# The first up-projection pair of MLP groups 2 to 6 by seven products instead of eight

## The chip, the cores and the metric

The kernel runs on one core of a Trainium2 chip. The metric is the time of one execution in microseconds (us), the median of several runs. Times inside an execution come from a hardware profile of one execution, the one whose page is shown.

The engines go by the profile's names: PE is TensorE (matmuls; PEld are its weight loads), DVE is VectorE, ACT is ScalarE, POOL is GpSimd, SP issues the DMAs from HBM. SBUF is the working memory, PSUM the eight banks that matmuls write. Each engine works through its own queue in order.

## The reference

Two decoder layers on 512 tokens of width 1024. What matters here is the squared-ReLU MLP that each layer has, with 4096 inner columns:

```python
def sq_relu_mlp(h, w_up, w_down):
    return jnp.square(jax.nn.relu(h @ w_up)) @ w_down

for i in range(DEPTH):              # DEPTH = 2
    ...                             # layer 0: attention, layer 1: gated convolution
    x = x + rmsnorm(m, g[1])
    f = sq_relu_mlp(rmsnorm(x, g[2]), w_mlp_up[i], w_mlp_down[i])
    x = x + rmsnorm(f, g[3])
    ...                             # gated per-layer embedding
```

All data is float32.

## The kernel before, in words

**Numbers in two parts.** Every matmul operand is split into a high part, rounded to the matmul's input type (`float32r`), and a low part, what is left. `split` (L274) makes them: ACT casts the high part (`wh`, `hTh`, `A11h`, ...), and DVE or POOL subtracts it from the source to give the low part (`wl`, ...). `mm3` (L266) then issues three matmuls for each product: high by high, low by high, high by low.

**The MLP in groups.** `mlp` (L957) takes the 4096 inner columns in eight groups of 512. In a group, `up` (L963) computes four column blocks of 128 (`f` = 0 to 3) for all 512 tokens: 8 row tiles of the weight by three matmuls, each 512 tokens wide. (Group 0 takes the tokens in two halves.) Then ACT takes the relu (`r`) and the square (`q`) of each block. `halves` and `quarters` split the squared blocks into the parts that the down-projection wants, after POOL has made sums of them (`s12`, `s34`).

**The down-projection by seven products.** In groups 0 to 6, `down` (L1003) uses Strassen's scheme already: the group's inner columns, tokens and output columns are halved, and seven products (`PRODUCTS`, in the order `STEPS` = 1, 2, 4, 5, 6, 7, 3) take the place of eight. The token side has parts A11, A12, A22 and sums S1 to S4; the weight side has B11, B21, B22 and differences T1 to T4, which POOL makes from the raw weights (tiles `dn_T...`). Each exists twice (p = 0 from column blocks 0 and 1, p = 1 from blocks 2 and 3), so a group has 8 differences on POOL and 14 forms to split: six straight from raw tiles on DVE, and the eight differences on POOL in groups above 0. Each product fills two PSUM banks, and DVE adds them to running sums (`acc`, L1021); group 0 copies them instead.

**What sets the order.** The weights are listed once, in the order of their use (`plan`, `plan_sums`). `prepare` runs ahead of the matmuls by a number of forms (`SOON` = 8): it fetches raw tiles on SP's queue (14 buffers, `RAWS`), lets POOL make the differences when their turn comes (`derive`), and issues the splits. A scheduler then lays out each engine's queue, PE's included. All tiles of 128x512 come from one pool of pages (`PAGES` = 70).

The convolution of layer 1 already uses the same scheme for two of its three projections (`sevens`), with 256 tokens a matmul and 128x512 weight forms. For it, the tail of layer 0 keeps an unsplit copy of the normed tokens in quarters B11, B12, B21, B22 (`full`), and DVE makes differences T1 to T4 of them.

Of the kernel before, what the change touches and what calls it, by code (L numbers as in the profile page):

```python
# [15 lines left out]
P = 128  # L16
D = 1024
S = 512
# [10 lines left out]
PAGES = 70  # L29
# [11 lines left out]
LATE = 0  # L41

# [26 lines left out]
def trunk(ctx: ExitStack, tc, x, xT, pT, g, gT, wv, wqk, bf, wo, wci, wcq, cw, wco, wup, wdn, wpp, wpg, out):  # L69
# [50 lines left out]
    def plan_down(l, gr):  # L120
# [10 lines left out]
                ((name, p), (a, p), (b, p), ALU.subtract)  # L131
                for p in range(2)
                for name, a, b in (("T1", "B12", "B11"), ("T3", "B22", "B12"),
                                   ("T2", "B22", "T1"), ("T4", "B21", "T2"))
# [3 lines left out]
    def plan_sevens(key, srcs):  # L138
        plan_sums(
            key,  # L140
            [(f,) for f in QUARTERS],
# [33 lines left out]
    def prepare(upto, lows=None):  # L175
        while begun[0] < min(upto, len(order)):
# [7 lines left out]
            if isinstance(at, tuple):  # L184
                raw, w = derived.pop(key), S
                eng = nc.gpsimd if (key[0] == "dn" and key[2] > 0) or key[-1] in ON_POOL else nc.vector
            else:
# [19 lines left out]
    for l in range(2):  # L207
# [25 lines left out]
        for gr in range(8):  # L233
            for i in range(2):
                for j in range(4):
                    plan(("up", l, 2 * gr + i, j), wup[l, 2 * gr + i, j])
# [37 lines left out]
    def split(hi, lo, src, eng=nc.vector):  # L274

        nc.scalar.copy(hi, src)  # L276
        return eng.tensor_tensor(out=lo, in0=src, in1=hi.bitcast(F32), op=ALU.subtract)  # L277

# [111 lines left out]
    def soon(t, n):  # L390

        return FEW if n else SOON
# [564 lines left out]
    def mlp(l, hT, xs, then, late):  # L957
# [5 lines left out]
        def up(gr, done, soon=lambda f: SOON):  # L963
            for lo, hi in ((0, 256), (256, 512)) if gr == 0 else ((0, 512),):
                n = hi - lo
                for f in range(4):
                    need(*range(lo // P, hi // P), *(range(NB) if f == 3 else ()))
                    ps = bank(f"up{l}_{gr}_{f}_{lo}")
                    for k in range(KT):
                        mm3(  # L970
                            ps[:, :n], narrow("up", l, 2 * gr + f // 2, k=k, c=f % 2 * P, soon=soon(f)),
# [4 lines left out]
                    done(f, lo, hi, r)  # L976

# [24 lines left out]

        def down(gr, A):  # L1003

            for i in STEPS:
                a_name, b_name = PRODUCTS[i]
# [34 lines left out]
        for gr in range(7):  # L1041
            A, s, q = {}, {}, {f: page(f"q{l}_{gr}_{f}") for f in range(4)}

            def done(f, lo, hi, r):
                square(q[f][:, lo:hi], r[:, : hi - lo])
                if lo == 0 and f % 2 == 0:
                    halves(gr, f, ("A11",), q[f], A)
# [3 lines left out]
            up(gr, done)  # L1051
            down(gr, A)
# [147 lines left out]
    xs = [load_x("xb", t) for t in range(NB)]  # L1200
    for l in range(2):
        if l == 1:
# [4 lines left out]
            kind, lhs, xs, g1, lambda t: pre_norm(t, xs[t], g2, hT, f"n2{l}"), opened  # L1207
# [19 lines left out]
        mlp(l, h2, xs, lambda t: pre_norm(t, xs[t], g4, hT, f"n4{l}"), late)  # L1227
        h4 = hT
        g5 = gain(l, 5)
        if l == 0:  # L1230
            g0 = gain(1, 0)
            hT = turned_x
            full = {}

            def quarters(t, n, ps):

                for q in range(2):
# [82 lines left out]
```

## Time and profile before

| | |
|---|---|
| runs (3) | 1218.8, 1220.0, 1220.02 us; median 1220.0 |
| span of the profiled execution, first to last instruction | 1216.5 us; no other time of it was kept, so what lies around the span is taken as 1220.0 - 1216.5 = 3.5 us |
| PE, DVE, ACT, POOL busy | 99%, 77%, 57%, 54% of the span |
| mean granted TensorE clock | 0.999 of full |

The rows of the profile are read as follows. A group row has line, engine, operation, output<-inputs, shapes and count; behind the bar stand busy time, mean ns of one, then the engine's idle time just before them and what ended it. A row of windows has the stretch, its length, and the busy time of each engine with its number of instructions, then granted clock, DMA share and GB/s. A timeline row has start and length in us of instructions of one kind that follow each other. In the profile of this kernel the up-projection's matmuls are `up`, the down-projection's `dn`.

### The profile page before, as it was taken

The numbers are of one execution on the slowest core, as the hardware profiler recorded it, in microseconds if no ns is written. First come the engines' busy times: TensorE is split into PE (matmuls) and PEld (weight loads), VectorE is DVE, ScalarE is ACT, GpSimd is POOL, SyncE is SP. The second block draws the span as 40 slices with busy tenths as digits, with TensorE's granted clock in tenths as the row PEclk, the third lists the DMA queues.
The fourth block names the chain that finished last, engine by engine and source line by source line (L and its number), as shares of the span: only waits on it lengthen the run. The fifth ranks groups of instructions, "written<-read, shape, count | busy, mean of one in ns | idle before, by whom it ended". The sixth has DMA issues, their size and how long they took to land.

```text
span 1216.5 us, 18743 instructions
## 1 busy us (share of the span) xinstructions
PE 1205.5 (99%) x6175; PEld 1027.5 (84%) x6175; DVE 931.4 (77%) x1474; ACT 691.4 (57%) x1465; POOL 655.4 (54%) x616
## 2 busy tenths in 40 slices
PE   9999999999999999999999999999999999999997
PEld 8888887898888888888889999989888888888886
DVE  7888889586669766879877888866876787669873
ACT  7687778458644564455665534545746445645551
POOL 2035666155787877774213455126676878678210
PEclk9999999999999999999999999999999999999999
DMA  9376544623234323438223123542422443135401
GB/s 333 122 210 172 167 152 125 222 93 94 77 113 138 102 66 110 139 97 276 83 88 108 35 80 103 176 154 71 139 87 65 127 138 106 61 112 185 162 13 58
DMA packets 87314, 150.84 MB, mean 124 GB/s; under 512 B 10352, under 2 KB 18080, under 8 KB 87216
## 3 DMA queue, kind: packets, MB, share of 16 engines
q1 hardware_dynamic: 86640, 149.11, 39.3%
q8 instruction: 49, 0.80, 0.3%
q10 hardware_dynamic: 576, 0.53, 0.1%
q14 instruction: 49, 0.40, 0.1%
HBM read 139.03 MB, written 6.37 MB: 120 GB/s over the span
## 4 chain that ended last, share of the span: by engine, by line
PE 91%; ACT 3%; issue 2%; DVE 2%; POOL 1%; DMA 0%; SPq 0%; POOLq 0%; DVEq 0%; ACTq 0%
PE up L269 9%; PE up L270 9%; PE up L268 9%; PE dn L268 8%; PE dn L270 8%; PE dn L269 8%; PE v L476 3%; PE pg L269 2%; PE pg L268 2%; PE pg L270 2%; PE qk L270 2%; PE qk L269 2%; PE qk L268 2%; PE pT L590 1%; PE co L269 1%
## 5 line engine op out<-in xcount | busy, mean ns | idle before, releaser
L277 DVE TENSOR_TENSOR wl<-raw,wh 128x512 fp32r<-128x512 f32 x346 | 344.7, 1041 | 14.1 <-ACT wh L276 13.4
L269 PE MATMUL up<-hTh,wl 128*128 128x512 f32 (+1 forms) x576 | 210.2, 365 | 0.0
L270 PE MATMUL up<-hTl,wh 128*128 128x512 f32 (+1 forms) x576 | 209.6, 365 | 0.0
L268 PE MATMUL up<-hTh,wh 128*128 128x512 f32 (+1 forms) x576 | 208.7, 366 | 0.0
L276 ACT CAST wh<-raw 128x512 fp32r<-128x512 f32 x346 | 189.4, 625 | 4.5 <-DVE xd L373 4.4
L975 ACT ACTIVATE r<-up 128x512 f32<-128x512 f32 (+1 forms) x72 | 39.5, 548 | 201.8 <-PE up L270 190.1
L277 POOL TENSOR_TENSOR wl<-dn_T,wh 128x512 fp32r<-128x512 f32 x96 | 132.7, 1416 | 30.0 <-ACT wh L276 30.0
L168 POOL TENSOR_TENSOR dn_T<-raw,raw 128x512 f32<-128x512 f32 x56 | 87.0, 1564 | 69.1 <-DMA raw<-in_wdn 50.5
L269 PEld LDWEIGHTS up<-hTh,wl 128*128 128x128 f32 x576 | 108.6, 189 | 17.5
L268 PEld LDWEIGHTS up<-hTh,wh 128*128 128x128 f32 x576 | 108.6, 189 | 17.5
L270 PEld LDWEIGHTS up<-hTl,wh 128*128 128x128 f32 x576 | 108.2, 189 | 17.4
L1021 DVE TENSOR_TENSOR acc<-dn,acc 128x512 f32<-128x512 f32 x168 | 107.4, 680 | 13.9 <-PE dn L270 13.9
L168 POOL TENSOR_TENSOR dn_T<-raw,dn_T 128x512 f32<-128x512 f32 x56 | 92.5, 1651 | 2.2
L276 ACT CAST wh<-dn_T 128x512 fp32r<-128x512 f32 x112 | 61.4, 616 | 10.9 <-POOL dn_T L168 10.9
L277 DVE TENSOR_TENSOR A12l<-q,A12h 128x512 fp32r<-128x512 f32 x28 | 23.2, 829 | 53.8 <-ACT A12h L276 53.8
L1035 POOL TENSOR_TENSOR acc<-acc,acc 128x512 f32<-128x512 f32 x28 | 46.9, 1707 | 9.9 <-DVE acc L1021 9.9
L277 DVE TENSOR_TENSOR A11l<-q,A11h 128x256 fp32r<-128x256 f32 x28 | 23.2, 828 | 36.5 <-ACT A11h L276 36.5
L270 PE MATMUL qk<-hTl,wh 128*128 128x512 f32 x128 | 50.7, 396 | 0.0
L269 PE MATMUL pg<-wh,hTl 128*128 128x512 f32 x128 | 50.5, 394 | 0.0
L268 PE MATMUL pg<-wh,hTh 128*128 128x512 f32 x128 | 50.4, 394 | 0.0
L268 PE MATMUL qk<-hTh,wh 128*128 128x512 f32 x128 | 50.3, 393 | 0.0
L269 PE MATMUL qk<-hTh,wl 128*128 128x512 f32 x128 | 50.2, 392 | 0.0
(404 smaller groups left out, 3304.5 us busy)
## 6 DMA issues: line engine op xcount, KB each, us to landing
raw<-in_wup SPq DMA_DIRECT2D x128, 256.0 KB, 2.9
raw<-in_wdn SPq DMA_DIRECT2D x128, 256.0 KB, 2.8
raw<-in_wcq SPq DMA_DIRECT2D x36, 256.0 KB, 2.8
raw<-in_wqk SPq DMA_DIRECT2D x32, 256.0 KB, 5.3
raw<-in_wpg SPq DMA_DIRECT2D x32, 256.0 KB, 4.1
g<-in_g SPq DMA_DIRECT2D x22, 256.0 KB, 5.9
prl<-neg_c SPq DMA_DIRECT2D x16, 256.0 KB, 6.3
raw<-in_wo SPq DMA_DIRECT2D x16, 256.0 KB, 4.7
```

The source lines that it names most:

```text
L168: ins = nc.gpsimd.tensor_tensor(out=B[name], in0=B[a], in1=B[b], op=op)
L268: nc.tensor.matmul(ps, a.hi, b.hi, start=start, stop=False)
L269: nc.tensor.matmul(ps, a.lo, b.hi, start=False, stop=False)
L270: nc.tensor.matmul(ps, a.hi, b.lo, start=False, stop=stop)
L276: nc.scalar.copy(hi, src)
L277: return eng.tensor_tensor(out=lo, in0=src, in1=hi.bitcast(F32), op=ALU.subtract)
L476: nc.tensor.matmul(ps[:, : V_CHUNKS[c][1]], getattr(of_x(k, t), p), getattr(ready["v", c, k], of), start=k == 0 and p == of, stop=k == KT ...
L590: nc.tensor.transpose(ps[:, b * P : (b + 1) * P], probs[h][b][:, j * P : (j + 1) * P], ident)
L975: nc.scalar.activation(r[:, :n], ps[:, :n], AF.Relu)
L1021: ins = nc.vector.tensor_tensor(out=a, in0=banks[s], in1=a, op=ALU.add)
L1035: nc.gpsimd.tensor_tensor(out=a, in0=a, in1=acc[i, s][:, :S], op=ALU.add)
```

## The change

In groups 2 to 6 of both layers, the column blocks 0 and 1 (the first pair) of the up-projection are computed by seven products, too. The weight side is the quartered 1024 x 256 block with forms A11, A12, A22, S1 to S4; the token side is the tokens' quarters B11, B21, B22 and differences T1 to T4. Each product is 4 x 3 matmuls of 256 tokens. Blocks 2 and 3 stay as they were.

- `plan_sevens` lists seven forms (in the order `UP_FORMS`) for the first pair's four raw tiles. POOL makes S1 to S4 of them (`up_..._S1` etc.), DVE makes all their low parts.
- `up_sevens` issues the products into three banks a, b, c. ACT copies the first product to `u`; DVE makes the sums `ud` and `uv` (512 wide), `ud`'s right half once more (256) and `um`. The relu of `d` and `m` is taken from SBUF, and `crossed` replaces `halves`/`quarters` for this pair: four POOL sums of 256 columns and four splits, as before in number.
- The token differences are made once for each layer (`token_sums`, on POOL, in the course of groups 0 and 1), and `pre_norm` ahead of each MLP keeps the unsplit quarters by 16 copies on ACT, as it did ahead of the convolution.
- In groups 2 to 6 the low parts of T4 and T1 of the down weights move from POOL to DVE (`ON_VECTOR`); T2's and T3's stay on POOL. In all groups POOL makes T1, T2, T4 ahead of T3.
- In groups 2 to 6 the order of PE's queue is the order of the code (`FIXED`), and the second pair's weights are prepared only 2 forms ahead (`SOON - BACK`), up to 4 after block 2 and 8 after block 3.
- `PAGES` goes from 70 to 77, with a smaller scratch area for DMA descriptors. The raw tiles of the first pair are laid out in quarters; the transfers are the same in number and size.

```diff
-PAGES = 70
+PAGES = 77
+BESIDE = range(2, 7)
+ON_VECTOR = ("T4", "T1")
+FIXED = range(2, 7)
+BACK = 6
+UP_SEVENS = range(2, 7)
+MORE = 0
+UP_FORMS = ("A11", "S2", "S1", "S3", "A12", "S4", "A22")
...
@@ prepare
                 eng = nc.gpsimd if (key[0] == "dn" and key[2] > 0) or key[-1] in ON_POOL else nc.vector
+                if key[0] == "up" or near(key) and key[3] in ON_VECTOR:
+                    eng = nc.vector
...
@@ the list of weights
+                tiles = [wup[l, 2 * gr + i, j] for j in range(4)]
+                if i == 0 and gr in UP_SEVENS:
+                    plan_sevens(("up", l, 2 * gr), tiles, UP_FORMS)
+                    continue
...
@@ mlp, up
+                    if f < 2 and gr in UP_SEVENS:
+                        if f == 0:
+                            done(f, 0, S, *up_sevens(gr))
+                        continue
...
-                            ps[:, :n], narrow("up", l, 2 * gr + f // 2, k=k, c=f % 2 * P, soon=soon(f)),
+                            ps[:, :n],
+                            narrow("up", l, 2 * gr + f // 2, k=k, c=f % 2 * P,
+                                   soon=SOON - BACK if gr in FIXED else soon(f)),
...
+                    if gr == 1:
+                        next(aside, None)
+                    if gr in FIXED:
+                        prepare(where["up", l, 2 * gr + 1, 3] + 1 + (SOON if f == 3 else SOON - BACK + 2))
+        def token_sums():
...
+                    nc.gpsimd.tensor_tensor(
+                        out=t, in0=full[a, q][:, :S], in1=full[b, q][:, :S], op=ALU.subtract
+                    )
+                    T[name, q] = Pair(*(page(f"{name}{s}{l}_{q}", F32R) for s in "hl"))
+                    split(T[name, q].hi[:, :S], T[name, q].lo[:, :S], t)
+                    yield
...
+        def up_sevens(gr):
+            L, R = slice(0, S // 2), slice(S // 2, S)
+            a, b, c = (bank(f"up{l}_{gr}_{s}") for s in "abc")
+            u, v, d, m = (page(f"u{s}{l}_{gr}") for s in "uvdm")
...
+            def product(ps, form, tokens):
+                for k in range(4):
+                    w = wide("up", l, 2 * gr, form, soon=SOON + MORE).at(lambda h: h[:, k * P : (k + 1) * P])
+                    mm3(ps, w, second(tokens, k), k == 0, k == 3)
+            product(c[:, L], "A11", "B11")
+            nc.scalar.copy(u[:, L], c[:, L])
+            product(a[:, R], "S2", "T2")
+            product(b[:, L], "S1", "T1")
+            product(b[:, R], "S3", "T3")
+            product(a[:, L], "A12", "B21")
...
+            add(two(d[:, :S]), two(a), both(u[:, L]))
+            add(two(v[:, :S]), two(b), both(d[:, R]))
+            add(d[:, R], b[:, L], v[:, R])
+            product(c[:, L], "S4", "B22")
+            product(c[:, R], "A22", "T4")
+            add(m[:, :S], c, v[:, :S])
...
+        def crossed(gr, d, m, A):
...
+            halves(gr, 0, ("A11", "A22"), d, A)
+            halves(gr, 0, ("A12",), m[:, R], A)
+            s12, s34 = page(f"s12{l}_{gr}_0"), page(f"s34{l}_{gr}_0")
+            sums(s12[:, L], m[:, L], d[:, R], ALU.add)
+            sums(s12[:, R], s12[:, L], d[:, L], ALU.subtract)
+            sums(s34[:, L], d[:, L], m[:, L], ALU.subtract)
+            sums(s34[:, R], m[:, R], s12[:, R], ALU.subtract)
+            halves(gr, 0, ("S1", "S2"), s12, A)
+            halves(gr, 0, ("S3", "S4"), s34, A)
...
@@ the groups
-            up(gr, done)
-            down(gr, A)
+            with ExitStack() as order:
+                if gr in FIXED:
+                    order.enter_context(tc.manual_schedule(engines={mybir.EngineType.PE}))
+                up(gr, done)
+                down(gr, A)
```

Three places in the queues, all in layer 0. In the names, `acc0_3_1<-dn0_3_31` is the last addition of group 3, `wl...` the low part of a weight form (from a `raw` tile or from a sum), and a 4 in the place of the group is group 4.

DVE at the start of group 4, before:

```order
L1021 TENSOR_TENSOR acc0_3_1_4308<-dn0_3_31_5507,acc0_3_1_4308 128x512
L277 TENSOR_TENSOR wl164_5572<-raw140_5539,wh164_5571 128x512
L277 TENSOR_TENSOR wl165_5582<-raw141_5541,wh165_5581 128x512
L277 TENSOR_TENSOR wl166_5592<-raw142_5543,wh166_5591 128x512
L277 TENSOR_TENSOR wl167_5602<-raw143_5545,wh167_5601 128x512
L277 TENSOR_TENSOR A11l0_4_0_5615<-q0_4_0_5534,A11h0_4_0_5614 128x256
L277 TENSOR_TENSOR A12l0_4_1_5649<-q0_4_1_5535,A12h0_4_1_5648 128x512
```

The same place now (two splits, of `raw138` and `raw139`, left out of the middle):

```order
L1123 TENSOR_TENSOR acc0_3_1_4374<-dn0_3_31_5720,acc0_3_1_4374 128x512
L293 TENSOR_TENSOR wl167_5708<-up_0_8_S4_5647,wh167_5707 128x512
L293 TENSOR_TENSOR wl168_5722<-raw135_5639,wh168_5721 128x512
L293 TENSOR_TENSOR wl169_5732<-raw136_5733,wh169_5731 128x512
L293 TENSOR_TENSOR wl170_5760<-raw137_5761,wh170_5759 128x512
...
L293 TENSOR_TENSOR wl173_5847<-raw140_5814,wh173_5846 128x512
L293 TENSOR_TENSOR wl174_5863<-raw141_5816,wh174_5862 128x512
L1038 TENSOR_TENSOR ud0_4_5757<-up0_4_a_5752,uu0_4_5755 128x512
L1038 TENSOR_TENSOR uv0_4_5756<-up0_4_b_5753,ud0_4_5757 128x512
L293 TENSOR_TENSOR wl175_5882<-raw142_5818,wh175_5881 128x512
L1038 TENSOR_TENSOR ud0_4_5757<-up0_4_b_5753,uv0_4_5756 128x256
L293 TENSOR_TENSOR wl176_5898<-raw143_5820,wh176_5897 128x512
L1038 TENSOR_TENSOR um0_4_5758<-up0_4_c_5754,uv0_4_5756 128x512
```

Where four splits of weights stood between the last addition and the first part of the squared blocks, there are ten, and the four sums of the seven products among and behind them.

DVE behind the last column block of group 4, before and now:

```order
L277 TENSOR_TENSOR S1l0_4_3_5751<-s120_4_3_5746,S1h0_4_3_5750 128x512
L1021 TENSOR_TENSOR acc0_1_0_4134<-dn0_4_10_5758,acc0_1_0_4134 128x512
L1021 TENSOR_TENSOR acc0_1_1_4136<-dn0_4_11_5759,acc0_1_1_4136 128x512
L277 TENSOR_TENSOR S3l0_4_3_5755<-s340_4_2_5712,S3h0_4_3_5754 128x512
L1021 TENSOR_TENSOR acc0_2_0_4160<-dn0_4_20_5782,acc0_2_0_4160 128x512
```

```order
L1123 TENSOR_TENSOR acc0_1_0_4164<-dn0_4_10_6036,acc0_1_0_4164 128x512
L293 TENSOR_TENSOR A12l0_4_3_6005<-q0_4_3_5749,A12h0_4_3_6004 128x512
L1123 TENSOR_TENSOR acc0_1_1_4166<-dn0_4_11_6037,acc0_1_1_4166 128x512
L293 TENSOR_TENSOR S1l0_4_3_6013<-s120_4_3_6008,S1h0_4_3_6012 128x512
L293 TENSOR_TENSOR S3l0_4_3_6017<-s340_4_2_5974,S3h0_4_3_6016 128x512
L293 TENSOR_TENSOR wl177_6021<-dn_0_4_T4_0_5834,wh177_6020 128x512
L293 TENSOR_TENSOR wl178_6025<-dn_0_4_T4_1_5840,wh178_6024 128x512
L1123 TENSOR_TENSOR acc0_2_0_4196<-dn0_4_20_6060,acc0_2_0_4196 128x512
```

T4's splits stand on DVE now, behind all parts of the last block; before, they stood on POOL between the sums of the two pairs. In layer 1 the addition `acc1_2_0` stands ahead of T4's first split.

POOL from the last sum of group 4 to the T sums of group 5, before and now:

```order
L989 TENSOR_TENSOR s340_4_2_5712<-q0_4_3_5537,s120_4_3_5746 128x256
L277 TENSOR_TENSOR wl172_5761<-dn_0_4_T2_0_5559,wh172_5760 128x512
L277 TENSOR_TENSOR wl173_5771<-dn_0_4_T2_1_5567,wh173_5770 128x512
L277 TENSOR_TENSOR wl174_5785<-dn_0_4_T3_0_5557,wh174_5784 128x512
L277 TENSOR_TENSOR wl175_5795<-dn_0_4_T3_1_5565,wh175_5794 128x512
L168 TENSOR_TENSOR dn_0_5_T1_0_5963<-raw160_5955,raw156_5947 128x512
```

```order
L1076 TENSOR_TENSOR s340_4_2_5974<-q0_4_3_5749,s120_4_3_6008 128x256
L293 TENSOR_TENSOR wl181_6039<-dn_0_4_T2_0_5832,wh181_6038 128x512
L293 TENSOR_TENSOR wl182_6049<-dn_0_4_T2_1_5838,wh182_6048 128x512
L293 TENSOR_TENSOR wl183_6063<-dn_0_4_T3_0_5842,wh183_6062 128x512
L293 TENSOR_TENSOR wl184_6073<-dn_0_4_T3_1_5844,wh184_6072 128x512
L178 TENSOR_TENSOR up_0_10_S1_6118<-raw150_6114,raw151_6116 128x512
L178 TENSOR_TENSOR up_0_10_S2_6120<-up_0_10_S1_6118,raw148_6110 128x512
L178 TENSOR_TENSOR up_0_10_S3_6122<-raw148_6110,raw150_6114 128x512
L178 TENSOR_TENSOR up_0_10_S4_6124<-raw149_6112,up_0_10_S2_6120 128x512
L178 TENSOR_TENSOR dn_0_5_T1_0_6307<-raw160_6299,raw156_6291 128x512
```

The four sums of the up weights have moved in ahead of the T sums.

79 lines of the change are left out of this document (57 added, 22 removed).

## Prediction

> **What bounds the kernel now.** I read the page's busy times and chain first, then the busy time by MLP group.
>
> ```profile
> span 1216.5 us, 18743 instructions
> PE 1205.5 (99%) x6175; PEld 1027.5 (84%) x6175; DVE 931.4 (77%) x1474; ACT 691.4 (57%) x1465; POOL 655.4 (54%) x616
> PE 91%; ACT 3%; issue 2%; DVE 2%; POOL 1%; DMA 0%; SPq 0%; POOLq 0%; DVEq 0%; ACTq 0%
> ```
>
> TensorE has work 99% of the time and carries 91% of the chain that ended last, so matmul time taken out comes off the span, provided that nothing else becomes late. Groups 2 to 6 of layer 0, one row each:
>
> ```profile
> core 0: us, PE busy (x) PEld busy (x) DVE busy (x) ACT busy (x) POOL busy (x), PEclk, DMA share, GB/s
> 336.15:376.95 40.80, 40.80 (x182) 33.79 (x180) 29.85 (x38) 20.83 (x38) 29.88 (x24) 1.00 0.35 103
> ...
> 417.75:458.55 40.80, 40.80 (x182) 33.80 (x180) 29.57 (x38) 20.83 (x38) 31.62 (x25) 1.00 0.36 108
> ...
> 499.35:540.15 40.80, 40.80 (x182) 33.79 (x180) 29.17 (x38) 20.84 (x38) 30.97 (x25) 1.00 0.35 104
> ```
>
> A group takes 40.80 us, TensorE is busy throughout, and VectorE has 11 us left over, GpSimd some 10, ScalarE 20. The clock is granted in full. The question is whether VectorE and GpSimd can hold a pace of 40.0 us with what the change gives them.
>
> **The gain on TensorE.** Spacing of the two matmul widths, from a stretch of each (the 96 up-matmuls of one group, and 48 of the 256-wide ones that the conv stage already runs; columns PE, PEld, ACT in the first row, PE, PEld, DVE, ACT, POOL in the second):
>
> ```profile
> 417.75:439.52 21.77, 21.77 (x96) 17.84 (x95) 1.79 (x3) 1.00 0.41 132
> 694.27:700.03 5.76, 5.76 (x48) 5.72 (x48) 0.00 (x0) 0.00 (x0) 0.29 (x1) 1.00 0.44 137
> ```
>
> That is 226.8 ns for 512 tokens and 120.0 ns for 256. One pair of column blocks costs 2 x 8 x 3 = 48 matmuls now, 48 x 0.2268 = 10.88 us, and 7 x 4 x 3 = 84 then, 84 x 0.120 = 10.08 us. The saving is 0.80 us, ten times (five groups, two layers): 8.0 us. The nominal group is 40.0 us. [...]
>
> **What VectorE and GpSimd get.** Their costs over the same five groups, VectorE, GpSimd and one row of ScalarE:
>
> ```profile
> L277 DVE TENSOR_TENSOR wl<-raw,wh 128x512 fp32r<-128x512 f32 x73 | 77.6, 1108 | 0.0
> L1021 DVE TENSOR_TENSOR acc<-dn,acc 128x512 f32<-128x512 f32 x70 | 44.8, 680 | 5.2 <-PE dn L270 5.2
> L277 DVE TENSOR_TENSOR A11l<-q,A11h 128x256 fp32r<-128x256 f32 x10 | 8.0, 801 | 14.9 <-ACT A11h L276 14.9
> L277 DVE TENSOR_TENSOR A12l<-q,A12h 128x512 fp32r<-128x512 f32 x10 | 7.9, 794 | 21.5 <-ACT A12h L276 21.5
> L277 DVE TENSOR_TENSOR S1l<-s,S1h 128x512 fp32r<-128x512 f32 x10 | 7.8, 777 | 12.4 <-ACT S1h L276 12.4
> L277 POOL TENSOR_TENSOR wl<-dn_T,wh 128x512 fp32r<-128x512 f32 x40 | 56.3, 1442 | 12.5 <-ACT wh L276 12.5
> L168 POOL TENSOR_TENSOR dn_T<-raw,dn_T 128x512 f32<-128x512 f32 x20 | 33.3, 1664 | 0.8
> L276 ACT CAST wh<-raw 128x512 fp32r<-128x512 f32 x70 | 37.0, 616 | 0.0
> ```
>
> The same operations, shortest/median/longest:
>
> ```profile
> L277 DVE TENSOR_TENSOR wl<-raw,wh x73: 673/1179/1779, 334.9 to 539.6; 128x512 fp32r<-128x512 f32 x73
> L277 POOL TENSOR_TENSOR wl<-dn_T,wh x40: 1287/1303/1815, 353.1 to 530.8; 128x512 fp32r<-128x512 f32 x40
> ```
>
> A split of a weight (two operands in SBUF) takes VectorE 0.67 us alone and up to 1.78; the addition to acc, of the same size but with one operand in PSUM, stays at 0.68. So the splits lose time to GpSimd and the additions do not. A start of a group shows it best, VectorE above, GpSimd below:
>
> ```profile
> 417.27 4.07 DVE L277 TENSOR_TENSOR wl<-raw,wh 128x512 fp32r<-128x512 f32 x3
> 421.27 2.47 DVE L1021 TENSOR_TENSOR acc<-dn,acc 128x512 f32<-128x512 f32 x4
> 423.66 5.21 DVE L277 TENSOR_TENSOR wl<-raw,wh 128x512 fp32r<-128x512 f32 x4
> 428.80 0.41 DVE L277 TENSOR_TENSOR A11l<-q,A11h 128x256 fp32r<-128x256 f32 x1
> 417.27 3.53 POOL L168 TENSOR_TENSOR dn_T<-raw,dn_T 128x512 f32<-128x512 f32 x2
> 420.76 2.99 POOL L168 TENSOR_TENSOR dn_T<-raw,raw 128x512 f32<-128x512 f32 x2
> 423.72 3.46 POOL L168 TENSOR_TENSOR dn_T<-raw,dn_T 128x512 f32<-128x512 f32 x2
> ```
>
> The seven splits take 9.28 us, 1.33 us each, while GpSimd's sums take 1.73 to 1.77 each (1.50 beside the additions): the two engines take turns, and a pair of them costs about 1.7 us.
>
> Per group the change adds to VectorE three more splits of up-weights (seven forms for four tiles), four splits of T4 and T1 that were GpSimd's, three 512-wide additions from PSUM and one 256-wide. At 0.67 and 0.68 that is 4.7 + 2.5 = 7.2 us, at 1.11 a split 10.3. On 29.9 us this gives 37.1 to 40.2 us, of 40.0. GpSimd gains four sums (S1 to S4) and gives up four splits: 4 x (1.66 - 1.44), about +0.9 us, 32 us of 40. ScalarE gains three casts and a shorter copy, at most 4 x 0.62 = 2.5 of 20 free us: hidden. No transfer is added, and the T sums' new order (T4 third, T3 last) moves none of them off GpSimd: nothing. The copies and token sums at the head of each layer fall into groups 0 and 1; I cost them at nothing, covered by the engines' spare time there, 0 to 2 us a layer if that cover is gone.
>
> **Where it becomes late: two places in each group.** Time t runs from the start of a group's up-projection.
>
> First, um, the last sum of the seven products. It stands on VectorE behind two additions to acc (the former group's last), ten weight splits and three sums (ud, uv, ud). Alone they would end at 0.2 + 2 x 0.68 + 10 x 0.67 + 3 x 0.68 + 0.41 = 10.7 us, just after the products (10.1). But GpSimd runs its eight T sums there, which it can start only after S4: at 1.7 us each to about t = 14, so that seven or eight of the ten splits meet one. At the 1.33 us of the quoted stretch um ends at 0.2 + 1.4 + 13.3 + 2.4 = 17.3. What hangs on it goes through ScalarE and GpSimd in order: two relus, two squares, four sums s12/s34, the cast of the last, and only then the relu, square and cast of column block 2, whose rows of the trace (a group's last block) are:
>
> ```profile
> 439.71 0.60 ACT L975 ACTIVATE r<-up 128x512 f32<-128x512 f32 x1 [2.48 <-PE up L270]
> 440.34 0.63 ACT L961 ACTIVATE q<-r 128x512 f32<-128x512 f32 x1
> 441.00 0.62 ACT L276 CAST A12h<-q 128x512 fp32r<-128x512 f32 x1
> 442.98 0.62 ACT L276 CAST S1h<-s 128x512 fp32r<-128x512 f32 x1 [1.35 <-POOL s L989]
> 443.80 0.62 ACT L276 CAST S3h<-s 128x512 fp32r<-128x512 f32 x1 [0.20 <-POOL s L989]
> 441.05 0.74 POOL L989 TENSOR_TENSOR s<-q,q 128x256 f32<-128x256 f32 x1 [0.97 <-ACT q L961]
> 441.66 0.69 DVE L277 TENSOR_TENSOR A12l<-q,A12h 128x512 fp32r<-128x512 f32 x1 [3.43 <-ACT A12h L276]
> ```
>
> From the end of um: 0.7 + 2 x 0.65 + 4 x 0.76 + 0.7 + 0.6 + 0.65 + 0.45 + 0.45 = 7.9 us until A11l of block 2 is there. TensorE wants it for the second half of the first down product, at 10.08 + 48 x 0.2268 = 20.97, plus 7 matmuls, 22.6. So um may end at 14.7 without a stall; at 17.3 TensorE waits 2.6 us. Bounds: no meeting, 0; all eight T sums at 1.1 us extra each, um at 19.5, 4.8 us.
>
> Second, T4. Its splits now follow on VectorE the whole chain of block 3 (by the rows above A12l ends 2.6 us after the block's relu starts, S3h at 4.7), in layer 1 also the addition of down product 2, whose first half TensorE ends no sooner than 21 matmuls (4.8 us) and some 0.2 us of handing over after the block's last matmul. With 0.68 for the addition and 0.67 for the split that is 6.3; TensorE wants T4's low part after 26 matmuls, at 5.9. It waits 0.4 to 0.6 us; if T1's split behind it meets GpSimd's T2, up to 1 us more. I take 0.5. Queued behind the waiting matmul is all the rest of TensorE, since its order is fixed in these groups.
>
> Sum per group: -0.8 + 2.6 + 0.5 = +2.3 us at the mean pace; the rows' durations overlap by some 0.06 us, over thirteen instructions ahead of um nearly a microsecond, and the stalls pass time in which the queues drain, so I take +2.0. Ten groups: +20 us. On the profiled span 1216.5 + 20 = 1236.5; the runs' median 1220.0 lies 3.5 us above that span, so 1240.
>
> **Rivals.** *Hidden anyway (faster).* Late splits cost nothing while um ends before 14.7. The conv stage shows VectorE and GpSimd both full with TensorE not waiting:
>
> ```profile
> 693.50:701.40 7.90, 7.90 (x68) 7.90 (x68) 7.87 (x9) 4.51 (x9) 7.90 (x5) 1.00 0.32 100
> ```
>
> Against it: that lasts 8 us, here it must hold for 40. It decides if no more than three or four of the ten splits meet a T sum; then 8.0 us less, 1212; with the T4 wait of 0.5 left, 1217.
>
> *A draw.* um in time, T4 and T1 wait 0.6 to 1.0 us a group: -8 + 6 to 10, 1218 to 1222.
>
> *The two engines never overlap (much slower).* If a split and a GpSimd operation shut each other out for their full length, a group needs 27 splits of 0.67, two of 0.41, GpSimd's sixteen of 1.29 and eight of 0.74: 18.1 + 0.8 + 20.6 + 5.9 = 45.4 us, against 40.8: +46 us, 1266. [...] By that rule the present group would need 20 x 0.67 + 0.8 + 26.5 = 40.7 of its 40.8 us, yet VectorE idles 11 and GpSimd 10 of them; and a pair of operations in turns takes 1.7 us, not 0.67 + 1.29 = 1.96. So the trace bears out the taking of turns, not its full length. By turns of 1.7 the need is 45.4 x 1.7 / 1.96 = 39.4 us of 40.0, which leaves a queue in order no room: the reason why I don't expect it hidden.
>
> **How the numbers follow.** Late by um and T4 0.55, at 1225 to 1258, likeliest 1240; full length 0.08, 1266; a draw 0.10; hidden 0.27, 1212 to 1217. Range: 1212 (a fifth of the hidden case left below it) to 1260. The likeliest case's own range is 1225 to 1258. About 0.2% (2.4 us) is what a measurement of this kernel tells from no change: faster 0.27, same 0.10, slower 0.63.
>
> **What would show it.** In the changed profile a group of 2 to 6 takes 42 to 43 us instead of 40.0; TensorE's waits in it stand ahead of the first down product (on A11h or A11l) and the third (on the T split); VectorE is busy over 38 us a group; weight splits average over 1.2 us; 256-wide up-matmuls lie 120 ns apart. I am wrong if um ends by t = 15, if GpSimd's T sums finish ahead of the group's start, if the ten splits ahead of um average under 1.0 us, or if the page pool (77 pages, of which the token sums and their parts hold 16 for the layer, against 70 before) makes casts wait for pages, which I price at nothing.

## The result and the profile after

The changed kernel takes 1313.8 us (median of four runs, 1313.2 to 1314.9), the kernel before 1220.0 (median of four): the ratio is 1.0777 (95% interval 1.0761 to 1.0792), 93.8 us longer. The forecast was 1240, at most 1260. The sign was right; the size was wrong by a factor of nearly five.

The page of the changed kernel, three lines:

```profile
span 1311.5 us, 19619 instructions
PE 1247.5 (95%) x6535; PEld 1048.3 (80%) x6535; DVE 1042.9 (80%) x1600; ACT 724.8 (55%) x1553; POOL 707.8 (54%) x632
PE 51%; DVE 13%; POOL 12%; issue 10%; ACT 9%; DMA 3%; SPq 0%; POOLq 0%; DVEq 0%; ACTq 0%
```

TensorE's share of the chain that ended last fell from 91% to 51%: its rate no longer sets the pace; chains over VectorE, GpSimd and ScalarE do. PE is busy 42 us longer although it has 8 us less to do, which goes with the lower clock: a mean of 0.981 of full speed was granted, 0.999 before.

Stretches of layer 0, columns as in the prediction (stretch, length, busy time of PE, PEld, DVE, ACT, POOL, clock, DMA share, GB/s): groups 3, 4 and 5, the first pair of group 3, and groups 0 and 1; below, groups 0 and 1 of before.

```profile
396.00:441.94 45.94, 42.71 (x217) 35.64 (x216) 39.97 (x46) 22.52 (x43) 32.23 (x25) 0.96 0.31 92
441.94:488.40 46.46, 43.15 (x218) 35.67 (x217) 39.83 (x50) 22.08 (x42) 32.14 (x24) 0.96 0.28 87
488.40:535.80 47.40, 43.92 (x217) 36.61 (x216) 40.84 (x49) 23.05 (x44) 33.69 (x26) 0.93 0.30 95
396.00:406.08 10.08, 10.08 (x86) 10.08 (x85) 10.08 (x8) 5.15 (x11) 9.77 (x7) 1.00 0.28 84
250.90:301.40 50.50, 47.15 (x294) 41.33 (x294) 39.63 (x43) 38.98 (x93) 34.25 (x30) 0.97 0.19 57
301.40:345.90 44.50, 42.25 (x182) 33.23 (x180) 22.36 (x35) 20.94 (x40) 39.40 (x28) 1.00 0.31 94
```

```profile
250.56:295.35 44.79, 44.66 (x294) 40.25 (x292) 30.66 (x38) 29.25 (x66) 23.17 (x23) 1.00 0.23 74
295.35:336.15 40.80, 40.80 (x182) 33.80 (x180) 31.58 (x34) 27.10 (x51) 31.99 (x26) 1.00 0.34 104
```

From the first matmul of one group to the first of the next, the ten changed groups take 46.0 to 52.4 us, 481.0 in all, against 408.0 before: +73.0 us. Groups 0 and 1 of both layers take 18.6 us more. The two profiled spans differ by 95.0 us, so 3.4 are left, 2.9 of them between group 6 of layer 0 and the MLP of layer 1. In the ten groups the spacing of the matmuls gives some 60 us of waits, some 20 us of matmuls at half clock, and the saving of 8.

TensorE's longest waits in the whole run (engine, line, releaser: us in all, times, longest):

```profile
PE dn L284 <- ACT A11h L292: 29.1, 10, 3.1
PE dn L286 <- DVE wl L293: 11.8, 15, 3.6
```

Group 4 of layer 0 on the timeline (start, length; in brackets the idle time before), t = 0 at 441.94. VectorE up to the last sum um, then GpSimd's T sums:

```profile
442.51 2.89 DVE L293 TENSOR_TENSOR wl<-up_S,wh 128x512 fp32r<-128x512 f32 x2
445.32 0.68 DVE L1123 TENSOR_TENSOR acc<-dn,acc 128x512 f32<-128x512 f32 x1
445.93 1.18 DVE L293 TENSOR_TENSOR wl<-raw,wh 128x512 fp32r<-128x512 f32 x1
447.03 0.68 DVE L1123 TENSOR_TENSOR acc<-dn,acc 128x512 f32<-128x512 f32 x1
447.63 1.18 DVE L293 TENSOR_TENSOR wl<-up_S,wh 128x512 fp32r<-128x512 f32 x1
448.73 8.68 DVE L293 TENSOR_TENSOR wl<-raw,wh 128x512 fp32r<-128x512 f32 x7
...
460.19 0.68 DVE L1038 TENSOR_TENSOR um<-up_c,uv 128x512 f32<-128x512 f32 x1
```

```profile
441.40 1.74 POOL L178 TENSOR_TENSOR dn_T<-raw,raw 128x512 f32<-128x512 f32 x1
443.23 3.33 POOL L178 TENSOR_TENSOR dn_T<-raw,dn_T 128x512 f32<-128x512 f32 x2
446.52 1.73 POOL L178 TENSOR_TENSOR dn_T<-raw,raw 128x512 f32<-128x512 f32 x1
448.33 3.32 POOL L178 TENSOR_TENSOR dn_T<-raw,dn_T 128x512 f32<-128x512 f32 x2
451.62 3.43 POOL L178 TENSOR_TENSOR dn_T<-raw,raw 128x512 f32<-128x512 f32 x2
```

The last addition to acc of group 3 ends at 447.71, t = 5.8, where the prediction had 1.6: three splits stand between the additions (442.51, two, and 445.93). The ten splits and three sums behind it take 13.2 us. um ends at 460.87, t = 18.9. Then ScalarE's relu, square and cast of block 2, TensorE's wait for that cast, and what follows the wait:

```profile
466.77 0.59 ACT L1001 ACTIVATE r<-up 128x512 f32<-128x512 f32 x1
468.06 0.41 ACT L292 CAST A11h<-q 128x256 fp32r<-128x256 f32 x1
468.51 0.50 PE L284 MATMUL dn<-wh,A11h 128*128 128x512 f32 x1 [3.09 <-ACT A11h L292]
470.36 0.63 PE L286 MATMUL dn<-wl,A11h 128*128 128x512 f32 x1
...
472.92 0.63 PE L286 MATMUL dn<-wl,A12h 128*128 128x512 f32 x1
```

The relu of block 2, whose matmuls ended at about t = 15.5, comes at t = 24.8, since it stands on ScalarE behind the whole chain that hangs on um. After the wait of 3.09 us the matmuls lie 427 ns apart instead of 227 from 470.36 to 473.34, half the clock: seven spacings, 1.4 us on top.

### The profile page after: what moved, and what is told of

It reads as the page before. It is cut to its first block, busy times and chain, and to the rows that moved or that the text cites. A ratio compares the mean times of both kernels' runs of the same rounds, so it can differ in the third digit from the quotient of the medians.

```text
span 1311.5 us, 19619 instructions
## 1 busy us (share of the span) xinstructions
PE 1247.5 (95%) x6535; PEld 1048.3 (80%) x6535; DVE 1042.9 (80%) x1600; ACT 724.8 (55%) x1553; POOL 707.8 (54%) x632
## 4 chain that ended last, share of the span: by engine, by line
PE 51%; DVE 13%; POOL 12%; issue 10%; ACT 9%; DMA 3%; SPq 0%; POOLq 0%; DVEq 0%; ACTq 0%
DVE wl L293 7%; PE dn L286 5%; PE dn L285 4%; PE dn L284 4%; POOL dn_T L178 3%; PE up L285 2%; POOL s L1076 2%; PE up L286 2%; PE up L284 2%; POOL wl L293 2%; ACT wh L292 2%; POOL s L1093 2%; PE qk L286 2%; POOL up_S L178 2%; PE qk L285 2%
## 5 line engine op out<-in xcount | busy, mean ns | idle before, releaser
L285 PE MATMUL up<-hTh,wl 128*128 128x512 f32 (+1 forms) x416 | 150.1, 362 | 0.4
L284 PE MATMUL up<-hTh,wh 128*128 128x512 f32 (+1 forms) x416 | 148.2, 358 | 1.8 <-ACT r L1001 1.8
L286 PE MATMUL up<-hTl,wh 128*128 128x512 f32 (+1 forms) x416 | 147.6, 357 | 0.0
L1123 DVE TENSOR_TENSOR acc<-dn,acc 128x512 f32<-128x512 f32 x168 | 110.3, 680 | 18.9 <-PE dn L286 18.9
L178 POOL TENSOR_TENSOR dn_T<-raw,raw 128x512 f32<-128x512 f32 x56 | 106.7, 1916 | 12.3 <-DMA raw<-in_wdn 9.1
L293 POOL TENSOR_TENSOR wl<-dn_T,wh 128x512 fp32r<-128x512 f32 x56 | 85.4, 1556 | 31.7 <-ACT wh L292 31.7
L285 PEld LDWEIGHTS up<-hTh,wl 128*128 128x128 f32 x416 | 78.5, 189 | 17.9 <-DVE wl L293 7.3
L284 PEld LDWEIGHTS up<-hTh,wh 128*128 128x128 f32 x416 | 78.5, 189 | 13.8 <-ACT r L1001 2.6
L286 PEld LDWEIGHTS up<-hTl,wh 128*128 128x128 f32 x416 | 78.3, 189 | 10.6
L293 DVE TENSOR_TENSOR wl<-dn_T,wh 128x512 fp32r<-128x512 f32 x56 | 68.4, 1260 | 0.0
L284 PE MATMUL dn<-wh,A11h 128*128 128x512 f32 x76 | 33.1, 444 | 29.5 <-ACT A11h L292 29.1
L293 DVE TENSOR_TENSOR wl<-up_S,wh 128x512 fp32r<-128x512 f32 x40 | 55.0, 1402 | 0.4 <-ACT wh L292 0.4
```

Source lines behind the costliest of these rows:

```text
L178: ins = nc.gpsimd.tensor_tensor(out=B[name], in0=B[a], in1=B[b], op=op)
L284: nc.tensor.matmul(ps, a.hi, b.hi, start=start, stop=False)
L285: nc.tensor.matmul(ps, a.lo, b.hi, start=False, stop=False)
L286: nc.tensor.matmul(ps, a.hi, b.lo, start=False, stop=stop)
L1123: ins = nc.vector.tensor_tensor(out=a, in0=banks[s], in1=a, op=ALU.add)
```

## The experiments

Each kernel is an edit of the changed one and was run once, beside one run of the kernel before (1218.8 to 1220.1 us on the four occasions). The four runs of the changed kernel lie within 1.8 us, and most steps discussed are 11 to 60 us; the two smallest, of about 6 us, are less sure.

**The frame without the seven products.** Everything but the seven products: written order, late preparation, moved splits, heads.

```diff
-UP_SEVENS = range(2, 7)
+UP_SEVENS = ()
```

> The seven products alone undone (all column blocks of groups 2 to 6 by eight products again); the fixed order of TensorE, T4's and T1's splits on VectorE, 77 pages, the token sums and copies at the head of each layer stay. Theory (VectorE's splits and GpSimd's sums take turns, so um is late): groups 2 to 6 fall from about 47.5 us to 41 to 42 (the wait for T4 stays), groups 0 and 1 keep their 9 us a layer; 1240 to 1250 us. Rival (the fixed order and the moved splits are the cost): the groups stay above 45 us and the time above 1290.

1306.65 us. Nearly the whole loss without a single new product: as the rival had it. What it means shows below, where the frame is taken apart.

**The T sums left out** in groups 2 to 6; the T forms are split straight from raw tiles.

```diff
+            if key[0] == "dn" and key[2] in UP_SEVENS:
+                derived[(*key, *name)] = derived.get((*key, *a)) or fetched[at[a]]
+                continue
             t = page("_".join(str(u) for u in (*key, *name)))
```

> GpSimd's eight T sums of the down weights left out in groups 2 to 6: T1 to T4 are a raw tile each, so the output is another; all splits and matmuls stay. Theory (taking turns): the ten splits ahead of um average near 0.7 us instead of 1.3, um ends by 13 us after the group's start, and the groups fall to 41 to 42 us; 1245 to 1260 us with the heads of the layers as they are. Rival (VectorE's added work in one queue is enough to make um late, GpSimd or not): groups above 45 us, over 1290.

1258.65 us: 55 us less. Group 4 takes 41.79 us, VectorE is down from 39.8 to 33.4, with nearly as many instructions:

```profile
430.99:472.78 41.79, 40.49 (x218) 34.72 (x216) 33.44 (x48) 22.59 (x42) 20.04 (x17) 1.00 0.33 100
```

VectorE's queue in this group, the last addition of the group before and um:

```profile
433.95 0.68 DVE L1126 TENSOR_TENSOR acc<-dn,acc 128x512 f32<-128x512 f32 x1
...
441.62 0.68 DVE L1041 TENSOR_TENSOR um<-up_c,uv 128x512 f32<-128x512 f32 x1
```

um ends at t = 11.3. The run shows that GpSimd's eight T sums are needed for the loss, but not whether by turns with the splits or by their place in GpSimd's queue.

**TensorE kept busy in the wait** by nine matmuls that nothing reads, so that the clock stays up.

```diff
+                    if i == 1 and p == 1 and gr in FIXED:
+                        idle = bank(f"idle{l}_{gr}")
+                        for _ in range(9):
+                            nc.tensor.matmul(idle, hT.hi[:, 0, :P], hT.hi[:, 0, :], start=True, stop=True)
```

> Nine matmuls of 512 columns into a bank that nobody reads are put in TensorE's fixed order ahead of the second half of the first down product, 2.0 us of work inside the 3.3 us wait for A11. Theory (a wait of over 3 us halves the granted clock for the 3.4 us behind it): the half-clock stretches of groups 2 to 6, 22 us in all, nearly vanish, and the time falls to 1292 to 1300. Rival (the slow matmuls behind the wait only hide the next wait, that for T4): the clock stays full but the waits for T4 grow by as much, 1308 to 1315.

1321.28 us. Group 4's clock is 1.00 instead of 0.96, and the group is 1.0 us longer:

```profile
445.07:492.53 47.46, 44.41 (x226) 36.04 (x225) 40.32 (x48) 22.50 (x43) 33.14 (x25) 1.00 0.29 89
```

The waits for a low part from VectorE, 11.8 us in the changed kernel, have grown:

```profile
PE dn L286 <- DVE wl L293: 22.4, 17, 3.0
```

So what the clock gives back (1.00 instead of 0.96) is spent at the next wait; this edit, at least, made no time of the full clock.

**Low parts from a copy in PSUM.** ScalarE copies each high part into a PSUM bank as well, and VectorE subtracts from there; additions with one operand in PSUM had not been slowed by GpSimd (680 ns in the mean in both kernels, groups 2 to 6 of layer 0).

```diff
+            elif eng is nc.vector and near(key) and w == S:
+                nc.scalar.copy(hi, raw)
+                other = bank(f"hi{n}")
+                nc.scalar.copy(other, hi.bitcast(F32))
+                nc.vector.tensor_tensor(out=lo, in0=raw, in1=other, op=ALU.subtract)
```

> In groups 2 to 6 ScalarE copies the high part of every weight that VectorE splits into a PSUM bank as well, and VectorE subtracts it from there: same number of VectorE operations, one operand less in SBUF; 21 more ScalarE copies of about 0.6 us a group. Theory (taking turns): these splits take 0.68 us whatever GpSimd does, um ends by 13, groups take 41 to 43 us, 1240 to 1260. Rival (plain load of VectorE): groups above 45, over 1290. Second rival (ScalarE, 23 + 13 us of a group, becomes late in its turn): splits at 0.68 us but the time still over 1290.

1319.23 us. The splits became quick beside GpSimd, and um early (t = 11), but the time did not fall:

```profile
L209 DVE TENSOR_TENSOR wl<-raw,hi 128x512 fp32r<-128x512 f32 x62 | 41.5, 680 | 17.5 <-ACT hi L208 17.5
```

```profile
PE dn L289 <- DVE wl L209: 47.3, 34, 4.8
```

L289 is the high by high matmul, which reads no low part: it waits for a PSUM bank that a copy still holds. So this run shows the turns (0.68 us a split instead of 1.21), but its edit brings a wait of its own.

**The frame taken apart**: four kernels, seven products on or off, and early preparation (BACK = 0), or scheduler's order (FIXED empty).

```diff
-BACK = 6
+BACK = 0
```

> BACK = 0: the seven products, the written order and the moved splits stay, but in groups 2 to 6 the weights of the down-projection are derived and split as far ahead as in the kernel before. Theory A (the late preparation sets the cost: T sums and the splits of T4 and T1 stand behind the group's own blocks in the queues of POOL, ACT and DVE): the ten groups fall from about 47 us to 42 to 44 us and the time to 1265 to 1285 us. Rival B (the splits and T sums that take turns set it, wherever they stand): the ten groups stay at 46 to 48 us and the time at 1300 to 1320 us.

> No group by seven products and BACK = 0: the written order of TensorE, the splits of T4 and T1 on VectorE and the heads stay. With BACK = 6 the same kernel took 1306.65 us. Theory A (late preparation): the ten groups fall from 45 to 46 us to about 41.5 us, 1240 to 1255 us in all, nearly all of what is left being the 18.6 us of the heads. Rival C (the written order of TensorE by itself, since the scheduler could no longer put a ready product ahead of one that waits): still 1290 us or more.

```diff
-FIXED = range(2, 7)
+FIXED = ()
```

> No group by seven products and no written order (FIXED empty, with which BACK has no effect): what stays is the token sums and copies at the heads of the layers, the splits of T4 and T1 on VectorE, the order of the T sums, 77 pages. Theories A and C: groups 2 to 6 are back at about 40.8 us and what is left is the heads' 18.6 us: 1236 to 1246 us. Rival D (the load of the moved splits on VectorE, or the pages, is the cost): 1260 us or more.

> The seven products with FIXED empty: the scheduler orders TensorE and the down-projection's weights are prepared as early as before. Theories A and C: ten groups of 41 to 43.5 us and the heads' 18.6 us: 1245 to 1270 us. Rival B (splits and T sums taking turns make the last sum of the seven products late, whatever the order): 1290 us or more. If this comes out well above the kernel with BACK = 0, the written order helped the seven products, and the late preparation alone harmed.

| | seven products | none |
|---|---|---|
| written order, BACK = 6 | 1313.8 | 1306.65 |
| written order, BACK = 0 | 1302.73 | 1247.71 |
| scheduler's order | 1304.27 | 1241.97 |

Without the seven products theory A holds: late preparation costs 59 us, the written order 5.7, the heads 22. With them it falls: early preparation gives back only 11 us, and the scheduler's order is no better, although its granted clock is 0.995 instead of 0.976. So the frame by itself (1306.65) had shown a different loss of like size. GpSimd's rows in it and with BACK = 0, group 3 beginning at 393.45 and 391.36:

```profile
411.07 2.53 POOL L178 TENSOR_TENSOR dn_T<-raw,raw 128x512 f32<-128x512 f32 x2
413.56 0.74 POOL L1076 TENSOR_TENSOR s<-q,q 128x256 f32<-128x256 f32 x1
```

```profile
395.11 3.04 POOL L178 TENSOR_TENSOR dn_T<-raw,raw 128x512 f32<-128x512 f32 x2
```

There the T sums end at t = 20.1 instead of 6.8, and the sums of the squared blocks queue behind them. In the changed kernel they end at t = 13.1: its first pair asks for weights eight forms ahead (`up_sevens`), without it the first pair is late, too. In the early order with the seven products, TensorE still waits 3 us in group 4 for the same cast. Its stretch, and ScalarE on the timeline:

```profile
444.35:489.64 45.29, 42.19 (x217) 35.91 (x216) 37.85 (x50) 22.57 (x42) 31.60 (x24) 0.96 0.29 93
```

```profile
460.11 0.63 ACT L1062 ACTIVATE rm<-um 128x512 f32<-128x512 f32 x1 [0.51 <-DVE um L1038]
...
466.00 2.17 ACT L292 CAST wh<-dn_T 128x512 fp32r<-128x512 f32 x4
468.07 0.59 ACT L1001 ACTIVATE r<-up 128x512 f32<-128x512 f32 x1
```

um is 3.2 us earlier there (t = 15.7; the group begins at 444.35), but four casts of T forms, 2.17 us, now stand between the chain and block 2's relu. That is where the gain of the early order went.

**The price of the seven products**, all in the early order (1302.73 us).

PSUM copies for the eleven up forms alone:

```diff
+            elif key[0] == "up" and near(key) and w == S:
...
```

> With BACK = 0 (1302.73 us as it is): in groups 2 to 6 the eleven up forms of a group get a second copy of the high part, made by ScalarE in a PSUM bank, and VectorE subtracts from there, so that these splits have one operand in PSUM and should cost 0.67 to 0.69 us beside GpSimd's sums, as they did when all of a group's splits had it. The down weights' splits stay in SBUF. Theory A (taking turns with GpSimd holds VectorE's queue back and makes um late): um ends near t = 11 to 13, the ten groups fall from 45 to 46 us to 40.5 to 43 us, 1250 to 1275 us in all, 22 us of the excess being the heads. Rival B (what is late is the sums' own chain through relu, square, GpSimd's four sums and the relu of block 2 on ScalarE, whose queue gets 11 more copies): 1290 us or more.

1269.13 us, 33.6 less. The ten groups fall from 468.1 to 418.7 us (-49.4); the two groups 1 rise by 17.8. Since the two groups 2 alone fall by 19.0, groups 1 and 2 together are hardly better off, and what is clearly won lies in groups 3 to 6: 364.8 us for the eight of them before this edit, 334.5 after it, 326.4 without the seven products. Groups 4 and 6 and group 1 of layer 0, the longest entry among TensorE's waits, and um on the timeline of group 4:

```profile
438.78:480.95 42.17, 40.73 (x217) 34.68 (x217) 30.45 (x49) 29.16 (x54) 28.14 (x25) 1.00 0.31 100
523.67:563.82 40.15, 40.15 (x217) 34.79 (x216) 31.56 (x48) 26.22 (x49) 21.07 (x19) 1.00 0.38 115
301.33:354.14 52.81, 43.87 (x181) 34.27 (x180) 26.55 (x41) 29.52 (x55) 47.46 (x34) 0.97 0.31 95
```

```profile
PE dn L289 <- DVE wl L209: 21.0, 10, 4.8
```

```profile
449.10 0.69 DVE L1043 TENSOR_TENSOR um<-up_c,uv 128x512 f32<-128x512 f32 x1
```

VectorE is busy 30 us a group instead of 38 for the same instructions, um ends at t = 11.0, and in group 6, which prepares no further up sums, the nominal 40.0 us are nearly reached (40.15). What is left is again the wait for banks.

The four sums of up weights left out (S forms split from raw tiles):

```diff
+            if key[0] == "up":
+                derived[(*key, *name)] = derived.get((*key, *a)) or fetched[at[a]]
+                continue
```

> With BACK = 0: the four sums S1 to S4 of the up weights are left out in groups 2 to 6 and their forms are split straight from raw tiles, so the output differs. The number of splits, matmuls and VectorE sums stays; GpSimd has 7 us less to do in a group, and its T sums can start that much earlier. Theory A (GpSimd's sums beside VectorE's splits): the groups fall from 45 to 46 us to 40 to 42.5 us, 1242 to 1265 us in all, as without the T sums. Rival B (VectorE's larger number of splits and sums by itself, or the chain behind um): 1285 us or more.

1271.62 us, 31.1 less, with VectorE's instructions unchanged: GpSimd's work, and not VectorE's number of operations alone, makes VectorE late. A little over the range that theory A gave.

T4's and T1's splits back on GpSimd:

```diff
-ON_VECTOR = ("T4", "T1")
+ON_VECTOR = ()
```

> With BACK = 0: the splits of T4 and T1 go back from VectorE to GpSimd, where they cost 1.29 us or more instead of 0.68. Theory A (the two engines together have no room): VectorE loses four splits, GpSimd gains four longer ones, which stand ahead of the sums for the next group: the same or worse, 1300 to 1325 us. Rival B (VectorE's queue alone is too long, 38 us of 40): um comes earlier by up to 2.7 us a group and the time falls to 1270 to 1290 us.

1319.96 us, 17.2 more. VectorE's queue alone is not the limit; a T form's split costs more on GpSimd (in the changed kernel 1.66 us in the mean there and 0.98 on VectorE, 20 each in groups 2 to 6 of layer 0).

The copies in a bank of their own, seven banks for matmuls, in the early and in the changed order:

```diff
-    psum = pool("psum", 8, space=PSUM)
+    psum, own = pool("psum", 7, space=PSUM), pool("own", 1, space=PSUM)
...
-                other = bank(f"hi{n}")
+                other = own.tile([P, S], F32, tag="own", name=f"hi{n}")
```

> BACK = 0 and the up forms' low parts subtracted from a copy in PSUM, as in the run that took 1269.13 us, but the copies have one PSUM bank of their own and the matmuls the other seven, so that no matmul waits for a bank that a copy holds. Theory A (turns are the price of the seven products): groups 2 to 6 at 40.0 to 41.5 us, group 1 back from 52.8 to about 44.5, 1236 to 1255 us in all, most of the excess at the heads. Rival B (a chain that remains once the splits are quick: the copies on ScalarE, which now wait for their one bank, or seven banks too few): 1265 us or more.

> The same in the changed kernel itself (BACK = 6). Theory A: without the turns what is left of the late preparation is a wait at T4: 11 us or less above the early order, 1240 to 1268 us. Rival B (late preparation costs its own 5 us a group, as it did without the seven products): 1285 us or more.

1302.32 and 1318.09 us: theory A's numbers missed in both. With one bank ScalarE and VectorE hand over at every split, which then costs 1.40 us, no less than a turn with GpSimd:

```profile
452.70 0.69 DVE L209 TENSOR_TENSOR wl<-raw,hi 128x512 fp32r<-128x512 f32 x1 [0.71 <-ACT hi L208]
454.11 0.69 DVE L209 TENSOR_TENSOR wl<-raw,hi 128x512 fp32r<-128x512 f32 x1 [0.71 <-ACT hi L208]
```

Seven banks also make the attention late (the first group's up-projection begins at 262.8 us instead of 251.7). The ten groups did fall, from 468.1 to 447.5 us in the early order, and the time lost elsewhere is as long. So these two did not take the turns away cheaply and do not decide the question; the run with eight banks says more.

**The heads.** The scheduler's order without the seven products (1241.97 us) once more, without the token sums:

```diff
-        aside = token_sums()
+        aside = iter(())
```

> The heads alone (no seven products in the up-projection, scheduler's order; 1241.97 us as it is), and in addition without the token sums T1 to T4 and their splits, which nothing uses there. What stays of the heads is the 16 copies of normed tokens on ScalarE for each layer. Theory A (the eight token sums on GpSimd, 1.73 us each, take turns with the weight splits of groups 0 and 1 and push the low parts behind them): 1220 to 1227 us. Rival B (the copies delay the normed tokens of the next block, and with them the first group): 1232 us or more.

1226.07 us: of the heads' 22 us the token sums and their splits are 15.9, the copies (with the pages and the moved splits) 6.1. Then with the sums on VectorE, without and with the seven products:

```diff
-                    nc.gpsimd.tensor_tensor(
+                    nc.vector.tensor_tensor(
                         out=t, in0=full[a, q][:, :S], in1=full[b, q][:, :S], op=ALU.subtract
```

> The heads alone (no seven products in the up-projection, scheduler's order; 1241.97 us with the token sums on GpSimd, 1226.07 without them), with the token sums on VectorE. A sum with both operands in SBUF costs VectorE about 0.67 us alone, against 1.73 us on GpSimd beside a split. Theory A (turns): 1227 to 1234 us. Rival B (the sums' splits and casts by themselves, or VectorE's longer queue): 1239 us or more.

> The copies in a bank of their own with BACK = 0, and the token sums of the heads made by VectorE instead of GpSimd. Theory A (the heads' price is turns, too): 8 to 15 us less than with GpSimd, 1224 to 1245 us: the copies of the normed tokens (6 us) are about what the seven products save (8 us), so that no gain over the kernel before is in sight. Rival B (VectorE has no room for eight more sums in groups 0 and 1): no less than with GpSimd.

1242.11 us, as with GpSimd, and 1301.09, 1.2 less. Theory A falls for the heads. Group 0 with the sums on GpSimd, on VectorE, and without them:

```profile
251.38:302.65 51.27, 47.13 (x293) 41.46 (x292) 40.22 (x44) 39.25 (x93) 34.54 (x30) 0.97 0.17 56
```

```profile
251.47:299.84 48.37, 45.65 (x294) 40.28 (x292) 34.69 (x46) 34.39 (x82) 22.98 (x23) 1.00 0.19 63
```

```profile
250.76:297.63 46.87, 44.57 (x293) 40.68 (x292) 33.10 (x42) 35.74 (x85) 24.92 (x24) 1.00 0.25 79
```

On VectorE GpSimd's part goes (VectorE is busy 34.69 us instead of 40.22, with the sums added) and group 0 is 2.9 us shorter, but group 1 is as much longer: the matmuls of group 2 begin at the same time within 0.4 us. That the sums cost 16 us in the heads is shown; which of their casts and splits delays what was not settled.

## Why the prediction was wrong

Step by step, the 93.8 us come together so: copies 6.1, token sums 15.9, written order 5.7, the seven products in the early order 55.0, late preparation 11.1. The order of the steps matters for the last two, as the table shows.

**The saving on TensorE** was right: group 3's 84 products lie in 10.08 us (row above). So was the place of the loss: ten waits ahead of the first down product. VectorE's 39.8 to 40.8 us a group and its splits' mean of 1.21 us (prediction: over 38, over 1.2) were right, too.

**The start of VectorE's queue failed**, and with it the time of um. The chain from um to A11l was right (7.9 predicted, 8.2 measured), and the ten splits and three sums were even quicker than I had them (13.2 against 15.7 us). But I let VectorE begin the group with two additions at t = 0.2 and end them at 1.6. In group 4 the last addition ends at 5.8, with three splits among the additions, and um came at 18.9, not 17.3. A row that the prediction quotes showed it: in group 4 of before, which begins at 417.75, four additions stand behind three splits, from 421.27 to 423.74, t = 3.5 to 6.0. There nothing urgent stood behind them. So this is the order of the queue and no backlog that the change brought; without GpSimd's T sums the last addition still ends at t = 3.6 (433.95 + 0.68, the group beginning at 430.99). What the T sums add is the length of the splits.

**The rest of the loss stood in terms that I had at or near nothing.** By the spacing of the matmuls, for the ten groups, with the forecast in brackets: the wait for block 2's A11h 30.8 us (26), slow matmuls and handing over behind it 24.0 (0), waits ahead of it in the group 12.3 (0), all later waits, T4's among them, 12.1 (5), the saving 8 (8). So the wait that um decides was missed by 5 us in all, the other waits and the clock by some 43. Groups 0 and 1 added 18.6 (0). A small one: what lies around the span, taken as 3.5 us, is 1.7 in runs that have both numbers (1220.1 and 1218.4).

**The clock was priced at nothing.** Some 20 us of half clock over the ten groups follow the waits. Nine of the ten waits for block 2's A11h, of 2.51 to 3.10 us, were followed by matmuls 427 ns apart instead of 227, at once or after up to 1.7 us of work; the stretch lasted 3.4 us in group 4, and in group 5, with a clock of 0.93, until some 6 us behind the wait. After the tenth, of 2.48 us, there was none; see below for shorter waits.

**The heads were priced at 0 to 2 us a layer** and cost 11. I counted spare time per group (VectorE 9 of 40.8 us in group 1 of before), not whose operands the added work stands ahead of.

**Written order and preparation were priced at nothing**, 5.7 and 11.1 us here, 59 for the second without the seven products. I took the order of the queues from the listing, but asked only what it does to T4 (0.5 us, which hardly showed in group 4), and not to the relu of block 2. The page pool, at nothing as well, was not tested by itself: the run with the copies alone (6.1 us) has the 77 pages, but not the token sums that fill them.

**The rival of full-length exclusion** gave 1266, nearer in size, but not for its reason. From t = -0.5 to 13.1 GpSimd's eight T sums fill 13.55 of 13.65 us, and in the same time VectorE makes about nine splits. If one engine shut the other out for its whole length, 8 x 1.29 + 9 x 0.67 = 16.3 us would be needed, by an estimate from the rows. The trace disagrees (13.65 us), as before; and a split with one operand in PSUM was not slowed (0.68 us in the mean of 62). Which mechanism makes the engines take turns is not shown.

Shown: that in groups 3 to 6 the turns are most of the seven products' price. There the eight groups take 38.4 us more than without the seven products, 44.8 with the saving of 6.4, and freeing eleven of the splits of a group takes off 30.3. In groups 1 and 2 the same edit moved the time from one to the other, and why the two groups 2 take longest in the early order was not settled. Not shown: a version without turns that keeps all its banks. None of the runs comes below the kernel before, and by their sums none would by much: with all turns gone, the saving of 8 us stands against copies of 6.1 and what is left of the token sums.

## What to carry to other kernels

A group that repeats begins with work of the group before it: read from the rows what still stands ahead in each queue at its start, before the deadline within it. When two engines each look three quarters busy, count how long an operation takes beside the other, not alone (here a split 1.21 us in the mean, 0.67 alone); with a need of 39.4 in 40 us, by the prediction's own estimate, a saving of 0.8 us on the bounding engine was bought with several. And give each wait of the bounding engine a price for the clock behind it (here 1.4 us behind a wait of 3.09). An experiment that undoes a part also changes the frame for the rest: here the frame alone lost as much as the whole change, for another reason, and only the two by three table told them apart.

## What the runs showed of the hardware

The clock fell to half after waits of 1.49 and 1.90 us, well under the 3.4 us of a slow stretch, and not after one of 2.48 us. In the early order with one bank for the copies, layer 0, group 5:

```profile
517.69 0.50 PE L289 MATMUL dn<-wh,A11h 128*128 128x512 f32 x1 [1.90 <-ACT A11h L297]
...
519.18 0.63 PE L290 MATMUL dn<-wh,A11l 128*128 128x512 f32 x1
```

A wait of 1.90 us was followed, 1.5 us after work had begun again, by 3.4 us at 427 ns a matmul, 1.6 us lost. In the frame without the seven products, layer 0, group 4, a wait of 1.49 us was enough for the same; in the changed kernel, layer 1, group 5, one of 2.48 us was not, and the matmuls behind it lie some 240 ns apart:

```profile
463.66 0.50 PE L284 MATMUL dn<-wh,A11h 128*128 128x512 f32 x1 [1.49 <-ACT A11h L292]
...
464.92 0.63 PE L284 MATMUL dn<-wh,A11h 128*128 128x512 f32 x1
```

```profile
1130.11 0.50 PE L284 MATMUL dn<-wh,A11h 128*128 128x512 f32 x1 [2.48 <-ACT A11h L292]
...
1131.34 0.40 PE L284 MATMUL dn<-wh,A11h 128*128 128x512 f32 x1
```

So the length of one wait does not tell by itself whether the clock falls; the wait of 1.90 us cost 3.5 us with the slow matmuls behind it, nearly twice its length.
